# One encoder layer on one core: a new order at the head, one output bank moved, norm statistics and final outputs re-timed

## The chip, the cores and the metric

The kernel runs on one core of a Trainium2 chip. A core has a matrix engine (TensorE, PE in the profile; its weight loads are listed as PEld), a vector engine (VectorE, DVE), an activation engine (ScalarE, ACT), a general engine (GpSimd, POOL) and a queue engine that mostly issues transfers (SyncE, SP). Each engine carries out its own list of instructions in the order of that list. Engines wait for each other by semaphores. The metric is the time of one execution on the device in microseconds (us).

## The reference

One layer of an encoder over 512 tokens of width 2048, in float32, followed by a last norm:

```python
xn = rms_norm(x, attn_norm_g[l])
proj = jnp.einsum("bsd,dc->bsc", xn, w_in[l])
u_val, u_gate, q, k, v = jnp.split(proj, split_pts, axis=-1)
y_conv = conformer_conv(u_val, u_gate, conv_dw_w[l], conv_dw_b[l], conv_ln_g[l], conv_ln_b[l])
...
y_na = neighborhood_attention(heads(q), heads(k), heads(v), rpb[l])
mixed = jnp.concatenate([rms_norm(y_conv, conv_out_g[l]), rms_norm(y_na, na_out_g[l])], axis=-1)
x = x + jnp.einsum("bsc,cd->bsd", mixed, w_out[l])
xn = rms_norm(x, ffn_norm_g[l])
up = jnp.einsum("bsd,df->bsf", xn, w_up[l])
up = depthwise_conv(up, ffn_dw_w[l], ffn_dw_b[l])
gate, val = jnp.split(up, 2, axis=-1)
x = x + jnp.einsum("bsf,fd->bsd", jax.nn.silu(gate) * val, w_down[l])
...
return rms_norm(x, final_norm_g)
```

`conformer_conv` is a gated linear unit, a depthwise convolution of width 31, a LayerNorm over 1024 channels and a swish. `neighborhood_attention` has 16 heads of width 64 on an 8 x 64 grid of tokens, each token looking at an 8 x 16 window. The MLP has 5632 hidden channels and a depthwise convolution of width 3 in its middle.

## The kernel before

**Layout.** Activations lie with channels on the 128 partitions and the 512 tokens along the free axis: x is 16 tiles of 128 x 512 (`KD` = 16). Weights come as raw units of 128 x 1024 float32 (512 KB) on SP's queue. Each product is made of three matmuls of a faster float32 form (`mm3`, lines 127 to 129): the weights are split into a high part `whi` (ACT, L116) and a low part `wlo` (DVE, L117), the activations likewise, and PE adds high x high, high x low and low x high. A unit of weights has one of four buffers (`NW` = 4): the split of a new unit writes where the fourth unit before it was, so it waits until PE has done with that one. Raw units have seven buffers.

**Order.** The program is written stage by stage, and a scheduler sets the order of each engine's list by dependencies and priority. `pin` keeps marked instructions in program order. `tick` moves a generator on by one `yield` behind a given matmul: so the steps of a norm (sum of squares, statistics, broadcast) are spread between the products of the stage in which they run. What is written later has lower priority, but an engine's list is fixed when the program is built.

**Banks.** PE writes to eight PSUM banks of 128 x 512: three that rotate under the tag `mm` (pool `psm`), one with the tag `po`, two that rotate as `tr`, and a pair `sc`.

**The stages the change touches**, in order of time:

- *Head* (lines 93 to 96, 214 to 255). ACT's queue loads the norm's factors g1 from the parameter array. DVE sets `ones` and casts it to `warm`; PE runs 20 idle matmuls on it, eight of full height (L236) and twelve of 64 rows (L240). SP's queue loads x tiles (L247) with the first weights of two column tiles (value and gate) between them, in pieces (`piece`, L225): one transfer of each tile at a time, 128 KB each at first. Each x tile is scaled by its factors and split: xh on ACT (L249), xl on DVE (L250). Then `project_first` multiplies both tiles, 16 steps of six matmuls.
- *Conv norms* (`group_a`). After the sums of the LayerNorm come two ticks, then its statistics `rln`; then eight swish tiles, then `RA_AFTER` = 2 more ticks, then the statistics `ra` of the group's RMS norm. Statistics are `rsqrt_steps`: matmuls with ones sum over the partitions (st, L190), DVE and ACT form the root (rsv, rsr, rsy), DVE builds a diagonal matrix in two parts (dg: L197 the high part, L201 four pieces of the low one), and one broadcast matmul for each part (st, L207) gives the factor of every token in a bank, which ACT copies out (L211).
- *Output projection*, first half (`out_half(ma, read_a)`). 16 groups of 24 matmuls, each group in the next of the three `mm` banks. `read_a` multiplies a finished group by ra (oa, L585) and adds it to x (L586). Until ra is there, groups wait in their banks. The last attention steps run between the groups: scores, softmax, weighted sum, squares of the result added to `accna` (L170).
- *First up-projection tile* (`up_apart(0, ...)`). Seven products of 24 matmuls over half the tokens each, from sums of weight quarters (ws, L666 to L677) and of x halves, which make up a fast matrix multiplication. The first three products start together; their results are read by ACT (vv, L823) and DVE (vl, L825). Product 6 is in the `po` bank, the others are in `mm` banks. The statistics of the MLP's norm (`rstd2`) run between the products.
- *Tail* (lines 918 to 998). The last output is written in two parts. For 384 of the 512 tokens, channels stay on partitions: `finish` multiplies each of the 16 x tiles by its gain and the token's factor and stores pairs; ten tiles are done on DVE from the broadcast's bank (fin, L935), six on POOL from its copy rb (L966, L933). For the last 128 tokens PE transposes, so that tokens lie on partitions, in four groups of 512 columns, g0 to g3: ACT sums squares (sq, L981), DVE multiplies by the final gains (xg, L984), and when the last group is done the root is formed (`root`, line 173) and the four xg are scaled by it and stored (out_N, L998). `spread(g, k)` hands out the `finish` calls over the groups: one after each step from (1, 0) on. PE's list has the groups in the order g0, g2, g1, g3.

Of the kernel before, what the change touches and what calls it, by code (L numbers as in the profile page):

```python
# [10 lines left out]
F32 = mybir.dt.float32  # L11
# [5 lines left out]
P = 128  # L17
D = 2048
# [36 lines left out]
RA_AFTER = 2  # L55

PCOLS = [("g1", KD), ("dww", NC_ * CK), ("dwb", NC_), ("lng", NC_), ("lnb", NC_), ("cog", NC_),
# [10 lines left out]
def layer(ctx: ExitStack, tc: tile.TileContext, xT, xG, w_in, w_v, w_out, w_up, w_down, par, tab, g3, out, last_out):  # L68
# [27 lines left out]
    pin(nc.scalar.dma_start(g1, par[:, POFF["g1"]:POFF["g1"] + KD]))  # L96
# [5 lines left out]

    ones_r = consts.tile([P, P], F32R, name="ones")
# [112 lines left out]
    early = [[], []]  # L216

    def piece(u, j, c0, c1):

        if c0 == 0:  # L220
            early[j].append((t4([P, U * P], "raw"), wpool.tile([P, U * P], F32R, tag="whi", name="whi", bufs=NW),
                             wpool.tile([P, U * P], F32R, tag="wlo", name="wlo", bufs=NW)))
        n = (NC_, 0)[j]
        raw, hi, lo = (t[:, c0 * P:c1 * P] for t in early[j][u])
        pin(nc.sync.dma_start(raw, w_in[n, :, (u * U + c0) * P:(u * U + c1) * P]))  # L225
        pin(nc.scalar.activation(hi, raw, AF.Copy))
        pin(nc.vector.tensor_sub(lo, raw, hi.bitcast(F32)))
# [4 lines left out]
    warm = t2("warm", F32R)  # L232
    pin(nc.vector.tensor_copy(warm.rearrange("p (i k) -> p i k", k=P), ones.unsqueeze(1).broadcast_to([P, S // P, P])))
    ps = psa.tile([P, 2, S], F32, tag="sc", name="idle")
    for n in (S, S) + 3 * (H,) + 3 * (H - 32,):
        pin(nc.tensor.matmul(ps[:, 0, :n], warm[:, :P], warm[:, :n], start=True, stop=True))  # L236
    for n in (S, S) + 4 * (H,):
        for j in range(2):
            rows = slice(j * DH, (j + 1) * DH)
            pin(nc.tensor.matmul(ps[:, j, :n], warm[rows, :P], warm[rows, :n], start=True, stop=True))  # L240


    pieces = {k: [(u, j, c0, c1) for j in range(2)]
              for k, u, c0, c1 in ((0, 0, 0, 2), (2, 0, 2, 4), (4, 0, 4, 8), (6, 1, 0, 4), (9, 1, 4, 8))}
    for k in range(KD):
        x1.append(t2("x"))
        last = pin(nc.sync.dma_start(x1[k], xG[k]))  # L247
# [4 lines left out]
        for c in pieces.get(k, ()):  # L252
            piece(*c)
# [118 lines left out]
    def group_a():  # L372
# [26 lines left out]
        for _ in range(RA_AFTER):  # L399
            yield  # L400
# [672 lines left out]
```

## Time and profile before

| | |
|---|---|
| median of 3 runs | 2029.9 us (2029.69 to 2030.85) |
| profiled execution | 2030.16 us |
| its span in the trace | 2028.4 us |
| PE busy | 2015.4 us, 99%, 10672 instructions |
| DVE busy | 1675.5 us, 83% |
| ACT busy | 1050.9 us, 52% |
| POOL busy | 159.5 us, 8% |
| bytes moved | 276.41 MB, mean 136 GB/s |

How to read it: the span runs from the first to the last instruction of the profiled execution, and its own time has 1.8 us around it. Busy times of different engines overlap. An idle time of an engine matters only where the chain of work that ended last runs through it. A matmul's bar in the trace is longer than its share of the time, since matmuls overlap; what counts is the distance between starts (0.23 us for 512 columns, 0.12 us for 256).

### The profile page before, as it was taken

Reading aid. Unit: us, or ns where it says so; the run is one execution under the profiler, and the core shown is the slowest. Engines: PE = TensorE matmul, PEld = TensorE weight load, DVE = VectorE, ACT = ScalarE, POOL = GpSimd, SP = SyncE. Lnnn points to the kernel's source line nnn. Section 1 sums busy time; section 2 is a strip of 40 time slices with the busy share of each in tenths; the row PEclk is TensorE's granted clock in tenths of the full one; section 3 lists DMA queues with packets and bytes.
Section 4 is the critical chain, followed back from the end, with each engine's and each line's share of the span. In section 5 each row is a group of like instructions: output and inputs, shape, how many; then the busy total and the mean of one; then the engine's idle time right before and its main releaser. Section 6 shows DMA issues by size and latency. Waiting matters only on the chain.

```text
span 2028.4 us, 28313 instructions
## 1 busy us (share of the span) xinstructions
PE 2015.4 (99%) x10672; PEld 1726.5 (85%) x10672; DVE 1675.5 (83%) x2298; ACT 1050.9 (52%) x1674; POOL 159.5 (8%) x188
## 2 busy tenths in 40 slices
PE   9999999999999999999999999999999999999998
PEld 7888888888888998888888888888888888888887
DVE  7986888988577898888888888888888888889875
ACT  7323344466346555555555555555555555555563
POOL 0000000000001001111111111111111111110111
PEclk9999999999999999999999999999999999999999
DMA  7232333336347435566565565565565565564583
GB/s 256 83 104 84 114 94 109 109 124 215 108 120 178 120 114 146 123 147 146 125 146 146 128 142 146 128 142 146 121 149 146 125 146 146 127 144 127 144 206 126
DMA packets 97784, 276.41 MB, mean 136 GB/s; under 512 B 10992, under 2 KB 12784, under 8 KB 97648
## 3 DMA queue, kind: packets, MB, share of 16 engines
q1 hardware_dynamic: 72288, 228.45, 36.3%
q0 software_dynamic: 25216, 46.15, 15.5%
q8 instruction: 84, 1.38, 0.3%
q14 instruction: 52, 0.43, 0.1%
q10 hardware_dynamic: 144, 0.01, 0.0%
HBM read 220.04 MB, written 54.53 MB: 135 GB/s over the span
## 4 chain that ended last, share of the span: by engine, by line
PE 96%; DVE 2%; DMA 1%; ACT 0%; issue 0%; SPq 0%; ACTq 0%; DVEq 0%
PE pu L718 25%; PE pu L724 13%; PE pd L129 8%; PE pd L127 8%; PE pd L128 8%; PE pj L127 5%; PE pj L128 5%; PE pj L129 5%; PE po L127 3%; PE po L128 2%; PE po L129 2%; PE pv L313 1%; PE pv L312 1%; PE pv L314 1%; PE pu L127 1%; PE pu L129 1%
## 5 line engine op out<-in xcount | busy, mean ns | idle before, releaser
L116 ACT ACTIVATE whi<-raw 128x1024 fp32r<-128x1024 f32 x364 | 384.4, 1058 | 503.8 <-PE pj L128 136.6
L117 DVE TENSOR_TENSOR wlo<-raw,whi 128x1024 fp32r<-128x1024 f32 x364 | 444.4, 1221 | 214.0 <-ACT whi L116 205.2
L718 PE MATMUL pu<-xc,whi 128*128 128x512 f32 x2240 | 552.9, 391 | 0.0
L718 PEld LDWEIGHTS pu<-xc,whi 128*128 128x128 f32 x2240 | 413.0, 188 | 79.1
L724 PEld LDWEIGHTS pu<-xc,wlo 128*128 128x128 f32 x2240 | 292.3, 191 | 13.9
L724 PE MATMUL pu<-xc,wlo 128*128 128x256 f32 x2240 | 296.6, 283 | 0.0
L129 PE MATMUL pd<-hh,wlo 128*128 128x512 f32 x640 | 250.1, 391 | 0.0
L127 PE MATMUL pd<-hh,whi 128*128 128x512 f32 x640 | 249.6, 390 | 0.0
L128 PE MATMUL pd<-hl,whi 128*128 128x512 f32 x640 | 249.3, 390 | 0.0
L871 POOL DMA_DIRECT2D x2d<-pdc x160 | 139.4, 873 | 1162.4 <-ACT pdc L870 837.4
L128 PE MATMUL pj<-xl,whi 128*128 128x512 f32 x512 | 200.2, 391 | 0.1
L129 PE MATMUL pj<-xh,wlo 128*128 128x512 f32 x512 | 200.0, 391 | 0.0
L127 PE MATMUL pj<-xh,whi 128*128 128x512 f32 x512 | 198.9, 393 | 0.0
L750 ACT ACTIVATE pl<-pu 128x256 f32<-128x256 f32 x280 | 104.6, 382 | 143.5 <-PE pu L718 136.4
L116 ACT ACTIVATE whi<-ws 128x1024 fp32r<-128x1024 f32 x132 | 139.8, 1059 | 75.2 <-PE pu L718 58.2
L366 DVE SCALAR_TENSOR_TENSOR y<-ch,prm,y 128x500 f32<-128x500 f32 (+14 forms) x240 | 173.3, 740 | 4.3
L117 DVE TENSOR_TENSOR wlo<-ws,whi 128x1024 fp32r<-128x1024 f32 x132 | 161.1, 1220 | 13.9 <-ACT whi L116 13.6
L129 PEld LDWEIGHTS pd<-hh,wlo 128*128 128x128 f32 x640 | 120.1, 188 | 28.5 <-DVE wlo L117 3.3
L128 PEld LDWEIGHTS pd<-hl,whi 128*128 128x128 f32 x640 | 120.2, 188 | 24.9 <-DVE hl L856 0.3
L127 PEld LDWEIGHTS pd<-hh,whi 128*128 128x128 f32 x640 | 120.4, 188 | 22.6
L870 ACT ACTIVATE pdc<-pd 128x512 f32<-128x512 f32 x160 | 93.8, 588 | 79.3 <-PE pd L129 65.9
L127 PEld LDWEIGHTS pj<-xh,whi 128*128 128x128 f32 x512 | 96.3, 188 | 20.7 <-ACT xh L249 0.2
(204 smaller groups left out, 2886.4 us busy)
## 6 DMA issues: line engine op xcount, KB each, us to landing
raw<-in_w_up SPq DMA_DIRECT2D x176, 512.0 KB, 3.7
raw<-in_w_down SPq DMA_DIRECT2D x88, 512.0 KB, 4.0
x2d<-pdc POOLq DMA_DIRECT2D x160, 256.0 KB, 4.8
raw<-in_w_in SPq DMA_DIRECT2D x60, 512.0 KB, 3.8
raw<-in_w_out SPq DMA_DIRECT2D x32, 512.0 KB, 3.8
raw<-in_w_v SPq DMA_DIRECT2D x16, 512.0 KB, 4.1
tab<-in_tab SPq DMA_DIRECT2D x32, 256.0 KB, 5.0
x<-in_xG SPq DMA_DIRECT2D x16, 256.0 KB, 5.4
```

Of the source, the lines that this page charges most:

```text
L116: i = nc.scalar.activation(hi[:, :n], raw[:, :n], AF.Copy)
L117: j = nc.vector.tensor_sub(lo[:, :n], raw[:, :n], hi[:, :n].bitcast(F32))
L127: nc.tensor.matmul(ps, hi[:, a], mh, start=start, stop=False)
L128: nc.tensor.matmul(ps, hi[:, a], ml, start=False, stop=False)
L129: return nc.tensor.matmul(ps, lo[:, a], mh, start=False, stop=stop)
L312: nc.tensor.matmul(ps, xh, wh[:, f], start=kk == 0, stop=False)
L366: nc.vector.scalar_tensor_tensor(y[:, a:b], h[:, a + j - PAD:b + j - PAD], prm[:, o + j:o + j + 1], y[:, a:b], op0=ALU.mult, op1=ALU.add)
L718: i = nc.tensor.matmul(ps, w[0][:, k * P:(k + 1) * P], comb[c][k], start=k == 0, stop=stop and k == ks[-1])
L724: i = nc.tensor.matmul(ps[:, H:], w[1][:, k * P:(k + 1) * P], comb[c][k][:, :H], start=False, stop=stop and k == U - 1)
L750: nc.scalar.activation(to, ps, AF.Copy)
L870: nc.scalar.activation(t, ps, AF.Copy)
L871: nc.gpsimd.dma_start(xd[d], t, accum_op=ALU.add)
```

## The change

- *Head.* The factors g1 leave the parameter array and are put behind the first x tile, in one array `x0` with it; one transfer brings both, and a copy on DVE puts the factors in their place. The transfer on ACT's queue goes. The first weights of the two tiles are interleaved in a new array `w_a`, so that one transfer brings the same steps of both; the pieces are those of steps 0 to 1, 2 to 3, 4 to 7, 8 to 11 and 12 to 15, issued behind x tiles 0, 1, 3, 7 and 11. xh of the first x tile is made by DVE, the others by ACT as before. `warm` is set by a memset, and the 20 idle matmuls become seven of full height (six of 512 columns, one of 256).
- *Conv norms.* Three ticks instead of two before `rln`; none instead of two before `ra`.
- *First up-projection tile.* For f = 0 the product in the `po` bank is product 3 instead of product 6.
- *Tail.* The second step of the statistics and the copy rb move from (1, 0) to (2, 2); from then on `finish` is called twice at each step instead of once. Two instructions are pinned, with which the order of PE's list stays g0, g2, g1, g3. The sum over the first three groups stands ahead of xg of g2. The root is written out with one step fewer between the square root and its result.

The instruction lists change with it. On PE, 13 idle matmuls go, and every real matmul stays. In the conv-norm stage, 35 matmuls of the output projection stand between the last conv-norm product and the next attention scores, where there were 24, and the broadcast for ra stands among them; on DVE the split of the weights that follow, and the sum into accna, stand ahead of the first oa, where the first oa stood ahead of both the next split and the adds to x. In the first up-projection tile both broadcast matmuls of rstd2 stand together behind the second tile's first product; on DVE the split of one more unit stands between the two parts of dg. In the tail, DVE's list has xg of g0 and xg of g1 ahead of the first fin, then six fin, the sum, xg of g2, four fin; ACT's list has rb behind sq of g1. ACT has one more activation table load (19 instead of 18).

```diff
--- before.py
+++ after.py
@@ -52,9 +52,8 @@
 ORDER = "aavaav" + "aq" * 4 + "qqqq"
 NORM_AT = 4
 NG = GW // 8
-RA_AFTER = 2
-
-PCOLS = [("g1", KD), ("dww", NC_ * CK), ("dwb", NC_), ("lng", NC_), ("lnb", NC_), ("cog", NC_),
+
+PCOLS = [("dww", NC_ * CK), ("dwb", NC_), ("lng", NC_), ("lnb", NC_), ("cog", NC_),
          ("nag", NC_), ("g2", KD), ("fww", 2 * NF * 3), ("fwb", 2 * NF), ("g3", KD)]
 POFF = {}
 _o = 0
...
@@ -93,13 +92,14 @@
     pin = tc.keep_in_program_order
 
     g1 = consts.tile([P, KD], F32, name="g1")
-    pin(nc.scalar.dma_start(g1, par[:, POFF["g1"]:POFF["g1"] + KD]))
     prm = consts.tile([P, NPAR], F32, name="prm")
 
     def pc(name, i):
         o = POFF[name] + i
         return prm[:, o:o + 1]
 
+    warm = t2("warm", F32R)
+    pin(nc.vector.memset(warm.bitcast(F32), 1.0))
     ones_r = consts.tile([P, P], F32R, name="ones")
     ones = ones_r.bitcast(F32)
     nc.vector.memset(ones, 1.0)
@@ -213,44 +213,49 @@
 
     xs, x1 = [], []
     acc1 = t2("acc1")
-    early = [[], []]
-
-    def piece(u, j, c0, c1):
-
-        if c0 == 0:
-            early[j].append((t4([P, U * P], "raw"), wpool.tile([P, U * P], F32R, tag="whi", name="whi", bufs=NW),
-                             wpool.tile([P, U * P], F32R, tag="wlo", name="wlo", bufs=NW)))
-        n = (NC_, 0)[j]
-        raw, hi, lo = (t[:, c0 * P:c1 * P] for t in early[j][u])
-        pin(nc.sync.dma_start(raw, w_in[n, :, (u * U + c0) * P:(u * U + c1) * P]))
-        pin(nc.scalar.activation(hi, raw, AF.Copy))
-        pin(nc.vector.tensor_sub(lo, raw, hi.bitcast(F32)))
+    early = []
+    xg0 = t4([P, U * P], "raw")[:, :S + KD]
+    pin(nc.sync.dma_start(xg0, x0))
+
+    def piece(k0, k1):
+
+        if k0 % CH == 0:
+            early.append((t4([P, U * P], "raw"), wpool.tile([P, U * P], F32R, tag="whi", name="whi", bufs=NW),
+                          wpool.tile([P, U * P], F32R, tag="wlo", name="wlo", bufs=NW)))
+        o = k0 // CH * U * P
+        pin(nc.sync.dma_start(early[-1][0][:, 2 * k0 * P - o:2 * k1 * P - o], w_a[:, 2 * k0 * P:2 * k1 * P]))
+        by = 2 if k0 else 1
+        for k in range(k0, k1, by):
+            raw, hi, lo = (t[:, 2 * k * P - o:2 * (k + by) * P - o] for t in early[-1])
+            pin(nc.scalar.activation(hi, raw, AF.Copy))
+            pin(nc.vector.tensor_sub(lo, raw, hi.bitcast(F32)))
 
 
     idle = consts.tile([P, 1], F32, name="idle")
     pin(nc.scalar.activation(idle, ones[:, 0:1], AF.Square))
-    warm = t2("warm", F32R)
-    pin(nc.vector.tensor_copy(warm.rearrange("p (i k) -> p i k", k=P), ones.unsqueeze(1).broadcast_to([P, S // P, P])))
     ps = psa.tile([P, 2, S], F32, tag="sc", name="idle")
-    for n in (S, S) + 3 * (H,) + 3 * (H - 32,):
+    for n in 6 * (S,) + (H,):
         pin(nc.tensor.matmul(ps[:, 0, :n], warm[:, :P], warm[:, :n], start=True, stop=True))
-    for n in (S, S) + 4 * (H,):
-        for j in range(2):
-            rows = slice(j * DH, (j + 1) * DH)
-            pin(nc.tensor.matmul(ps[:, j, :n], warm[rows, :P], warm[rows, :n], start=True, stop=True))
-
-
-    pieces = {k: [(u, j, c0, c1) for j in range(2)]
-              for k, u, c0, c1 in ((0, 0, 0, 2), (2, 0, 2, 4), (4, 0, 4, 8), (6, 1, 0, 4), (9, 1, 4, 8))}
+
+    pieces = {0: (0, 2), 1: (2, 4), 3: (4, 8), 7: (8, 12), 11: (12, 16)}
     for k in range(KD):
-        x1.append(t2("x"))
-        last = pin(nc.sync.dma_start(x1[k], xG[k]))
+        if k:
+            x1.append(t2("x"))
+            last = pin(nc.sync.dma_start(x1[k], xG[k - 1]))
+        else:
+            x1.append(xg0[:, :S])
         h, l = t2("xh", F32R), t2("xl", F32R)
-        pin(nc.scalar.activation(h, x1[k], AF.Copy, scale=g1[:, k:k + 1]))
-        pin(nc.vector.scalar_tensor_tensor(l, x1[k], g1[:, k:k + 1], h.bitcast(F32), op0=ALU.mult, op1=ALU.subtract))
+        g = g1[:, k:k + 1] if k else xg0[:, S:S + 1]
+        if k:
+            pin(nc.scalar.activation(h, x1[k], AF.Copy, scale=g))
+        else:
+            pin(nc.vector.tensor_scalar(h, x1[k], g, None, op0=ALU.mult))
+        pin(nc.vector.scalar_tensor_tensor(l, x1[k], g, h.bitcast(F32), op0=ALU.mult, op1=ALU.subtract))
         xs.append((h, l))
-        for c in pieces.get(k, ()):
-            piece(*c)
+        if k in pieces:
+            piece(*pieces[k])
+        if k == 0:
+            pin(nc.vector.tensor_copy(g1, xg0[:, S:]))
     with tc.issue_after(last.ins):
         nc.sync.dma_start(prm, par)
     a_, q_, v_ = iter(range(NC_)), iter(range(NP_)), iter(range(2))
@@ -331,7 +336,7 @@
         both = [psa.tile([P, S], F32, tag="tr", name="pj", bufs=2) for _ in range(2)]
         for kk in range(KD):
             for j in range(2):
-                m = mm3(both[j], early[j][kk // U][1:], kk % U, xs[kk][0], xs[kk][1], kk == 0, kk == KD - 1)
+                m = mm3(both[j], early[kk // CH][1:], kk % CH * 2 + j, xs[kk][0], xs[kk][1], kk == 0, kk == KD - 1)
             if kk % 4 == 3:
                 tick(m)
         return both
@@ -385,8 +390,8 @@
             sum_sq(acc, ys[i], i == 0)
             if i == NC_ // 2 - 1:
                 yield
-        yield
-        yield
+        for _ in range(3):
+            yield
         r = yield from rsqrt_steps(acc, CONV, "rln")
         acc = t2("acc")
         for i in range(NC_):
@@ -396,8 +401,6 @@
             sum_sq(acc, ys[i], i == 0)
             if i % 2:
                 yield
-        for _ in range(RA_AFTER):
-            yield
         ra.append((yield from rsqrt_steps(acc, CONV, "ra")))
 
 
@@ -793,7 +796,7 @@
     def up_apart(f, between):
 
         def begin(c):
-            return weights(), (psa.tile([P, S], F32, tag="po", name="pu") if c == 6 else
+            return weights(), (psa.tile([P, S], F32, tag="po", name="pu") if c == (6 if f else 3) else
                                psm.tile([P, S], F32, tag="mm", name="pu"))[:, :H]
 
         def part(c, w, ps, ks):
@@ -956,38 +959,45 @@
     def spread(g, k):
         if (g, k) == (0, 1):
             next(stats)
-        elif (g, k) == (1, 0):
+        elif (g, k) == (2, 2):
             try:
                 next(stats)
             except StopIteration as e:
                 rb.append(e.value)
-            finish(pairs.pop(0), rb[0], split=True)
             rb.append(t2("rb")[:, fm])
             nc.scalar.activation(rb[1], rb[0], AF.Copy)
-        elif rb and pairs:
-            at = pairs.pop(0)
+        for at in pairs[:2 if rb else 0]:
+            pairs.remove(at)
             finish(at, rb[at % 3 == 1], at % 3 == 1, at % 3 != 1)
 
     for g, ps in enumerate(banks):
         for i in range(CH):
-            nc.tensor.matmul(ps[:, i * P:(i + 1) * P], x2[g * CH + i][:, tm], ident, start=i == 0, stop=False,
-                             is_transpose=True)
+            m = nc.tensor.matmul(ps[:, i * P:(i + 1) * P], x2[g * CH + i][:, tm], ident, start=i == 0, stop=False,
+                                 is_transpose=True)
+            if g == CH - 1 and i == 0:
+                pin(m)
         for k in range(n):
             (hh, hl), (dh, dl) = hs[k], ws[g * CH + k]
-            nc.tensor.matmul(ps, hh[:, tm], dh, start=False, stop=False)
+            i = nc.tensor.matmul(ps, hh[:, tm], dh, start=False, stop=False)
+            if (g, k) == (2, 3):
+                pin(i)
             nc.tensor.matmul(ps, hl[:, tm], dh, start=False, stop=False)
             nc.tensor.matmul(ps, hh[:, tm], dl, start=False, stop=k == n - 1)
             spread(g, k)
         nc.scalar.activation(t2("sq"), ps, AF.Square, accum_out=sums[:, g:g + 1])
+        if g == CH - 2:
+            nc.vector.tensor_reduce(v, sums[:, :CH - 1], axis=AX.X, op=ALU.add)
+            nc.vector.tensor_scalar(v, v, 1.0 / D, EPS, op0=ALU.mult, op1=ALU.add)
         xg.append(t2("xg"))
         if g < CH - 1:
             nc.vector.tensor_mul(xg[g], ps, gains[g])
-        if g == CH - 2:
-            nc.vector.tensor_reduce(v, sums[:, :CH - 1], axis=AX.X, op=ALU.add)
-            nc.vector.tensor_scalar(v, v, 1.0 / D, EPS, op0=ALU.mult, op1=ALU.add)
     assert not pairs
     nc.vector.scalar_tensor_tensor(v, sums[:, CH - 1:], 1.0 / D, v, op0=ALU.mult, op1=ALU.add)
-    root(r, y, v)
+    nc.scalar.activation(r, v, AF.Sqrt)
+    nc.vector.tensor_scalar(v, v, -0.5, None, op0=ALU.mult)
+    nc.vector.reciprocal(r, r)
+    nc.vector.scalar_tensor_tensor(y, r, v, r, op0=ALU.mult, op1=ALU.mult)
+    nc.vector.scalar_tensor_tensor(y, y, 1.5, r, op0=ALU.add, op1=ALU.mult)
     for g in range(CH):
         if g == CH - 1:
             nc.vector.scalar_tensor_tensor(xg[g], banks[g], y, gains[g], op0=ALU.mult, op1=ALU.mult)
@@ -1016,8 +1026,10 @@
     a = {n: np.asarray(v) for n, v in inputs.items()}
     xT = np.ascontiguousarray(a["x"][0].T).reshape(KD, P, S)
     xG = np.ascontiguousarray(xT.reshape(KD, P, WH, NG, 8).transpose(0, 1, 3, 2, 4)).reshape(KD, P, S)
+    x0, xG = np.concatenate([xG[0], _cols(a["attn_norm_g"][0])], axis=1), np.ascontiguousarray(xG[1:])
     wi = a["w_in"][0]
     w_in = np.ascontiguousarray(_units(wi[:, :2 * CONV + 2 * NA]))
+    w_a = np.stack([w_in[n].reshape(P, KD, P) for n in (NC_, 0)], axis=2).reshape(P, -1)
     w_v = np.ascontiguousarray(wi[:, 2 * CONV + 2 * NA:].reshape(KD // 2, 2, P, 2, S).transpose(3, 0, 2, 1, 4)
                                ).reshape(2, KD // 2, P, 2 * S)
     wo = a["w_out"][0]
...
```

More of the change, by code (lines that the diff above doesn't have):

```diff
@@ L67, in layer @@
 @with_exitstack
-def layer(ctx: ExitStack, tc: tile.TileContext, xT, xG, w_in, w_v, w_out, w_up, w_down, par, tab, g3, out, last_out):
+def layer(ctx: ExitStack, tc: tile.TileContext, xT, xG, x0, w_a, w_in, w_v, w_out, w_up, w_down, par, tab, g3, out, last_out):
     nc = tc.nc
@@ L1058 @@
     tab = np.ascontiguousarray(tab.transpose(0, 2, 1, 3))
-    arrays = {"xT": xT, "xG": xG, "w_in": w_in, "w_v": w_v, "w_out": w_out, "w_up": w_up, "w_down": w_down,
+    arrays = {"xT": xT, "xG": xG, "x0": np.ascontiguousarray(x0), "w_a": np.ascontiguousarray(w_a), "w_in": w_in, "w_v": w_v, "w_out": w_out, "w_up": w_up, "w_down": w_down,
               "par": np.ascontiguousarray(par), "tab": tab,
```

1 line of the change is left out of this document (removed).

## The prediction

> **What bounds the kernel now.** I read the page first, then all waits of the matmul engine, then the timeline at each of them.
>
> ```profile
> span 2028.4 us, 28313 instructions
> PE 2015.4 (99%) x10672; PEld 1726.5 (85%) x10672; DVE 1675.5 (83%) x2298; ACT 1050.9 (52%) x1674; POOL 159.5 (8%) x188
> PE 96%; DVE 2%; DMA 1%; ACT 0%; issue 0%; SPq 0%; ACTq 0%; DVEq 0%
> ...
> PE idle L236 <- DVE warm L233: 1.6, 1, 1.6
> PE pu L127 <- ACT vv L823: 1.5, 1, 1.5
> PE st L190 <- DVE acc L170: 0.3, 1, 0.3
> PE po L127 <- DVE oa L585: 0.3, 1, 0.3
> ```
>
> The chain that ends last is 96% TensorE (PE), and PE is busy 99% of the span. The change drops 13 idle matmuls and no real one, so it can gain only at the start, in PE's few waits (1.5, 0.3 and 0.3 us after the start) and behind PE's last matmul. Against that, each wait that a new instruction order makes on PE lengthens the run in full. So I laid the changed kernel's order on each engine against the old one and walked through the four places where they differ, with durations of the old trace. The profiled execution took 2030.16 us (1.8 us around its span); the median of the runs is 2029.9, 0.26 less. 0.2% of it, 4.1 us, is about what a measurement here can tell from no change: "same" means 2025.8 to 2034.0.
>
> **The head.** Columns of a timeline: start, duration, engine, line, operation; in brackets the engine's idle time and what ended it.
>
> ```profile
> 1.65 2.47 PE L236 MATMUL idle<-warm 128*128 128x512 f32 x8 [1.65 <-DVE warm L233]
> ...
> 4.39 0.40 ACT L226 ACTIVATE whi<-raw 128x256 fp32r<-128x256 f32 x1
> ...
> 5.52 0.42 ACT L226 ACTIVATE whi<-raw 128x256 fp32r<-128x256 f32 x1 [0.73 <-DMA raw<-in_w_in]
> ...
> 6.05 0.80 PE L127 MATMUL pj<-xh,whi 128*128 128x512 f32 x1
> 6.64 0.63 PE L128 MATMUL pj<-xl,whi 128*128 128x512 f32 x1
> 7.07 0.63 PE L129 MATMUL pj<-xh,wlo 128*128 128x512 f32 x1
> 7.50 0.51 PE L127 MATMUL pj<-xh,whi 128*128 128x512 f32 x1
> 7.85 0.39 PE L128 MATMUL pj<-xl,whi 128*128 128x512 f32 x1
> 8.08 0.40 PE L129 MATMUL pj<-xh,wlo 128*128 128x512 f32 x1
> ```
>
> The first real matmul (6.05) waits for the second tile's first weights: they land at 5.5, the first tile's by 4.39. Matmul starts lie 0.59, 0.43, 0.43 and 0.35 us apart, then 0.23: PE runs at half speed until about 7.7, six microseconds after its first idle matmul. Now both tiles' first weights come in one 256 KB transfer, directly behind the x tile that brings its factors along. I bound its landing by these two rows, so the first real matmul starts between 6.05 - 1.13 = 4.92 and 6.05. Started at 4.92 with the switch still at 7.7, 1.13 us of half-speed work is won, worth half, 0.6. If the denser idle matmuls also bring the switch ahead of all real work, the excess of the four gaps over 0.23 (0.36 + 0.20 + 0.20 + 0.12 = 0.9) goes too: 1.13 + 0.9 = 2.0 won. In the other direction, seven idle matmuls (about 0.59 + 5 x 0.43 + 0.2 = 2.9 us from 1.4) end at 4.3, and PE pauses. If the six microseconds counted from the first real matmul, half speed would last to 10.9 or 12.1 instead of 7.7: 1.0 to 2.2 lost. I take **-0.6**, the case nearest to the rows (-2.0 to +2.2). The factor transfer that goes from ACT's queue, the cast that becomes a memset and xh of the first tile moving to DVE all lie in the time in which PE runs idle matmuls; uncovered, the last would add 0.7.
>
> **Conv norms and output projection.** One more tick before the first conv norm (rln) removes the wait of L190 (0.3). Without RA_AFTER the second one's factor (ra) is ready before the projection's second group, where it was read late.
>
> ```profile
> 497.83 0.58 ACT L507 ACTIVATE ao<-po 128x512 f32<-128x512 f32 x1
> 498.44 0.63 ACT L169 ACTIVATE sq<-ao 128x512 f32<-128x512 f32 x1
> 499.11 0.69 DVE L170 TENSOR_TENSOR accna<-accna,sq 128x512 f32<-128x512 f32 x1 [0.25 <-ACT sq L169]
> 500.47 1.29 DVE L585 TENSOR_TENSOR oa<-po,ra 128x512 f32<-128x512 f32 x2 [0.67 <-ACT ra L211]
> 500.57 0.39 PE L129 MATMUL po<-mah,wlo 128*128 128x512 f32 x1
> 500.77 1.06 ACT L116 ACTIVATE whi<-raw 128x1024 fp32r<-128x1024 f32 x1 [0.33 <-PE po L128]
> 501.22 0.50 PE L127 MATMUL po<-mah,whi 128*128 128x512 f32 x1 [0.26 <-DVE oa L585]
> 503.48 1.21 DVE L117 TENSOR_TENSOR wlo<-raw,whi 128x1024 fp32r<-128x1024 f32 x1
> ```
>
> PE's fourth output group (501.22) takes the bank of the first, which DVE frees with oa. In the old order oa stands ahead of the next weight split, at 500.47, and PE waits 0.26. In the new order eleven more projection matmuls stand ahead of the next attention step's scores, which come 11 x 0.23 = 2.5 us later, and DVE has that step's softmax, then wlo, then accna, and only then oa. This wlo belongs to weights whose buffer (four in turn) is the one that the third group has just used. So nothing on that path can start before PE finishes the third group: whi 1.06, wlo 1.21, accna 0.69 (its square follows whi by 0.58 + 0.63, as late as wlo), oa 0.69, together 3.65, less about 0.3 of overlap, plus hand-overs: **3.5** of wait on PE, with the rest of PE's list behind it. Lower bound 0, if the buffers came free another way. Less the 0.3 and 0.3 removed: **+2.9** (-0.6 to +3.2). The moved statistics themselves (st, dg, st) end 1 to 2 us ahead of PE by the same walk. One more activation table load lies on ACT, busy 52%.
>
> **First up-projection tile.**
>
> ```profile
> 678.80 0.28 PE L129 MATMUL pu<-xc,wlo 128*128 128x256 f32 x1
> ...
> 680.61 0.39 PE L127 MATMUL pu<-xc,whi 128*128 128x256 f32 x1 [1.53 <-ACT vv L823]
> ...
> 693.11 0.28 PE L127 MATMUL pu<-xc,whi 128*128 128x256 f32 x1
> 693.44 0.47 PE L207 MATMUL st<-dg,ones 128*128 128x512 f32 x1
> ...
> 694.35 1.13 DVE L201 SCALAR_TENSOR_TENSOR dg<-ident,rsy,dg 128x128 fp32r<-128x128 f32 x4
> ...
> 695.66 0.40 PE L207 MATMUL st<-dg,ones 128*128 128x512 f32 x1
> ```
>
> Product 3 gets a bank that is free, so the gap of 678.80 to 680.61 shrinks to the usual 0.12: 1.69 won. In the old order PE reaches the first broadcast (st) at 693.2, waits 0.2, and the second stands 16 matmuls behind it, which covers L201. In the new order both stand together at the end of the second tile's first product, about 694.1 (23 matmuls later, 1.9 sooner), and on DVE another wlo stands between the two factors (dg). Its whi needs the buffer of that very product: from its end run whi 1.06, wlo 1.21, L201 1.13, about 3.4 with the hand-over, before PE may do the second st; the first st fills 0.23 of it, some 1.5 us in, since L197 stands behind three splits and two weight sums. Cost 3.2, less 1.69 and 0.2: **+1.3** (-1.9 to +2.5).
>
> **The clock in these waits.** Windows: columns are busy time with counts of PE, PEld, DVE, ACT, POOL, then the granted clock.
>
> ```profile
> 2019.40:2021.50 2.10, 0.00 (x0) 0.00 (x0) 1.58 (x9) 0.86 (x3) 1.00 (x2) 1.00 1.02 380
> 2021.60:2028.40 6.80, 0.00 (x0) 0.00 (x0) 1.17 (x3) 1.34 (x2) 0.00 (x0) 0.50 0.79 295
> ```
>
> About 2.2 us after PE's last matmul its clock fell to half; the old waits, up to 1.5, were shorter. A 3.5 us wait is longer than that, and by the head it may take up to six microseconds of work to leave half speed: 0 to 3.0 lost. I take half of it for the unbroken wait, **+1.5**, and **+0.8** for the broken one (pieces of 1.5 and 1.7 us), 0 to 3.0 each. The Trainium skill, "TensorE: Matmul & The Clock Gate", Part 1, has the clock fall only after a whole idle window of about 3.4 us, of a free-running grid. By that rule a 3.5 us wait would seldom hold such a window and the clock term would be nearly 0, which is the second rival below; the row has it fall after 2.2.
>
> **The tail.**
>
> ```profile
> 2012.77 1.14 DVE L935 SCALAR_TENSOR_TENSOR fin<-x,prm,st 128x384 f32<-128x384 f32 x2 [0.87 <-PE st L207]
> 2014.52 5.88 POOL L933 TENSOR_TENSOR fin<-x,rb 128x384 f32<-128x384 f32 x6 [39.61 <-ACT rb L966]
> 2016.51 0.60 ACT L981 ACTIVATE sq<-pt 128x512 f32<-128x512 f32 x1 [2.07 <-PE pt L979]
> 2017.23 0.69 DVE L984 TENSOR_TENSOR xg<-pt,g3b 128x512 f32<-128x512 f32 x1
> 2017.84 1.66 DVE L935 SCALAR_TENSOR_TENSOR fin<-x,prm,st 128x384 f32<-128x384 f32 x3
> 2020.45 0.16 DVE L989 SCALAR_TENSOR_TENSOR rsv<-rsl,rsv 128x1 f32<-128x1 f32 x1
> 2021.66 0.49 DVE L997 TENSOR_SCALAR xg<-xg,rsy 128x512 f32<-128x512 f32 x1
> ```
>
> Ten fin outputs run on DVE, from 2012.77 on, six on POOL, from 2014.52. In the new order xg of group g1 stands on DVE ahead of all of them, and it needs PE's end of g1 (2016.5, where sq starts); on ACT rb, which POOL needs, stands behind that sq. So DVE stands still from about 2012 to 2016.5. Then: xg to 2017.1, six fin at 0.54 to 2020.4, reduce and xg of g2 to 2021.2, four fin to 2023.4, then the root, which loses one small step (0.2): 1.21 - 0.2 = 1.0 from the variance to L997, so L997 starts at 2024.4, **+2.8**. POOL, started at 2017.7, ends by 2023.6 and isn't later. What follows L997 I leave as it was. Lower bound -0.2 (fin hidden after all), upper +3.5 (outputs bunch in the queues).
>
> **Sum.** -0.6 + 2.9 + 1.3 + 1.5 + 0.8 + 2.8 = +8.7 on 2030.16 gives 2038.9, against the median 2038.6.
>
> **Rivals.**
> - *The order does no harm* (the splits and fin come in time, as they did): -0.6 - 0.6 - 1.9 - 0.2 = -3.3, **2026.6**; with the best head 2025.2. For it: the old kernel's lists, of the same length, cost PE 2 us in all. Against it: in both stages the wait closes on itself, since the split ahead needs PE's latest product.
> - *The clock holds*: the same without the clock terms, +6.4, **2036.3**.
> - *One of the three costs is absent* (tail, bank or broadcast): +8.7 less 2.8, 5.0 or 4.0, **2033.4 to 2035.6**.
> - *Slower still: half speed lasts.* Each wait costs the full 3.0, and the head's pause adds 2.2 in place of -0.6: **2045**. It decides if the clock needs the whole six microseconds anew.
> - *The change doesn't do what it says at the head*: the common transfer lands no sooner than 5.5; +0.6, **2039.2**, which the forecast's range holds.
>
> **How the numbers follow.** Forecast with its near range (2036.5 to 2042, the slow head in it) 0.47; clock holds 0.17; one cost absent 0.15; no harm 0.13; half speed lasts 0.08. The range of 2031.5 to 2043.5 leaves out most of "no harm" and of the last one, about 0.2. Slower than 2034.0: 0.47 + 0.17 + 0.08 + half to two thirds of 0.15, about 0.81; faster only with the best head in "no harm", 0.04; same 0.15.
>
> **What would show it.** PE waits of about 3.5 us at a projection matmul near 500 us with oa as releaser, and at a broadcast st near 694 with dg as releaser; no wait on vv near 679; matmul starts 0.4 apart behind either wait if the clock falls; the first fin on DVE behind an xg, five microseconds after its st; the first real matmul at 4.9 to 6.0. I'm wrong if PE's waits add up to under 3 us, or if the last outputs leave no later after PE's last matmul than now.

## The result and the profile after

The changed kernel takes 2040.51 us (median of 6 runs, 2039.91 to 2041.58), beside 2030.38 for the old one on the same chip (6 runs, 2029.69 to 2030.85): a ratio of 1.005, 95% interval 1.0037 to 1.0063, so about 10 us slower. Beside the experiments further down, 27 of 90 runs of the old kernel took 2031.2 to 2034.3 us and the others 2029.3 to 2030.7, so the means of its runs lie 0.5 to 0.8 above their medians. The profiled execution of the changed kernel took 2040.10 us, with this span, these busy times and this chain of work (the page of the changed kernel):

```profile
span 2038.3 us, 28283 instructions
PE 2016.6 (99%) x10659; PEld 1727.7 (85%) x10659; DVE 1676.5 (82%) x2299; ACT 1050.1 (52%) x1673; POOL 159.6 (8%) x188
PE 97%; DVE 1%; DMA 1%; issue 0%; SPq 0%; ACT 0%; ACTq 0%
```

The summary looks like that of the old kernel: PE is still 99% busy, and it is 1.2 us more busy although 13 idle matmuls are gone. The loss of 9.9 us in the span can't be read here. It shows in PE's waits (engine, its line, what it waited for: us in total, times, longest):

```profile
engine line waited for: us in total, times, longest us
PE po L127 <- DVE oa L588: 3.4, 1, 3.4
PE st L207 <- DVE dg L201: 1.6, 1, 1.6
PE idle L238 <- DVE warm L102: 1.5, 1, 1.5
PE st L207 <- DVE dg L197: 1.4, 1, 1.4
PE pj L127 <- ACT whi L230: 0.4, 1, 0.4
```

The wait on vv (1.5) and the two of 0.3 are gone; in their place stand 3.4 behind oa, and 1.4 + 1.6 behind the two halves of dg. Where the time goes along the run is seen by counting PE's real matmuls in both traces and comparing the starts of those that have equally many before them:

| | before, us | after, us | after - before |
|---|---|---|---|
| first real matmul | 6.05 | 4.98 | -1.07 |
| with 48 before it | 18.29 | 17.64 | -0.65 |
| with 2650 before it, behind the moved ra | 529.24 | 532.18 | +2.94 |
| with 3700 before it, behind the first up-projection tile | 719.76 | 725.43 | +5.67 |
| last | 2018.94 | 2024.62 | +5.68 |
| end of the span | 2028.39 | 2038.33 | +9.94 |

So there are four terms: the head -0.65, the conv-norm stage +3.6, the first up-projection tile +2.7, and what lies behind PE's last matmul +4.3. Between them nothing moves: the 1300 us of MLP behind the 3700 matmuls add 0.01. Here is each place in the timeline of the changed kernel, in selected rows (start, duration, engine, line, operation, idle time and releaser). The head:

```profile
1.46 3.14 PE L238 MATMUL idle<-warm 128*128 128x512 f32 x7 [1.46 <-DVE warm L102]
...
4.51 0.72 ACT L230 ACTIVATE whi<-raw 128x256 fp32r<-128x256 f32 x2 [2.27 <-DMA raw<-in_w_a]
4.98 0.80 PE L127 MATMUL pj<-xh,whi 128*128 128x512 f32 x1 [0.38 <-ACT whi L230]
```

The common transfer has landed by 4.5; real work starts 1.07 us sooner, and PE's idle matmuls end only 0.38 before it. The conv-norm stage:

```profile
499.01 0.39 PE L129 MATMUL po<-mah,wlo 128*128 128x512 f32 x1
499.21 1.06 ACT L116 ACTIVATE whi<-raw 128x1024 fp32r<-128x1024 f32 x1 [0.98 <-PE po L128]
500.18 0.58 ACT L510 ACTIVATE ao<-po 128x512 f32<-128x512 f32 x1
500.30 1.22 DVE L117 TENSOR_TENSOR wlo<-raw,whi 128x1024 fp32r<-128x1024 f32 x1 [0.60 <-ACT whi L116]
500.79 0.63 ACT L169 ACTIVATE sq<-ao 128x512 f32<-128x512 f32 x1
501.45 0.69 DVE L170 TENSOR_TENSOR accna<-accna,sq 128x512 f32<-128x512 f32 x1
502.06 1.28 DVE L588 TENSOR_TENSOR oa<-po,ra 128x512 f32<-128x512 f32 x2
502.80 0.79 PE L127 MATMUL po<-mah,whi 128*128 128x512 f32 x1 [3.40 <-DVE oa L588]
503.39 0.63 PE L128 MATMUL po<-mal,whi 128*128 128x512 f32 x1
503.81 0.63 PE L129 MATMUL po<-mah,wlo 128*128 128x512 f32 x1
```

The factor ra itself has been ready since 486.3 (L211). Read from top to bottom this is the loop: PE ends the third group; that frees a weight buffer for whi; wlo follows whi; accna follows its square, which stands behind whi on ACT; oa follows accna; and oa frees the bank that PE needs. Behind the wait the matmuls start 0.59 and then 0.43 apart instead of 0.23. The first up-projection tile:

```profile
697.03 0.28 PE L129 MATMUL pu<-xc,wlo 128*128 128x256 f32 x1
697.28 1.06 ACT L116 ACTIVATE whi<-ws 128x1024 fp32r<-128x1024 f32 x1 [1.82 <-PE pu L128]
697.84 0.68 DVE L197 TENSOR_TENSOR dg<-ident,rsy 128x512 fp32r<-128x512 f32 x1
698.45 1.22 DVE L117 TENSOR_TENSOR wlo<-ws,whi 128x1024 fp32r<-128x1024 f32 x1
698.67 0.47 PE L207 MATMUL st<-dg,ones 128*128 128x512 f32 x1 [1.36 <-DVE dg L197]
699.58 1.13 DVE L201 SCALAR_TENSOR_TENSOR dg<-ident,rsy,dg 128x128 fp32r<-128x128 f32 x4
700.77 0.79 PE L207 MATMUL st<-dg,ones 128*128 128x512 f32 x1 [1.63 <-DVE dg L201]
```

The split (698.45) stands between the two parts of dg, and its whi (697.28) waited for the very product that has just ended. And the tail, with PE's broadcast (L207) and rows of DVE, ACT, POOL and SP's queue:

```profile
2016.88 0.68 DVE L993 TENSOR_TENSOR xg<-pt,g3b 128x512 f32<-128x512 f32 x1
2017.39 0.51 PE L207 MATMUL st<-dg,ones 128*128 128x384 f32 x2
...
2021.84 0.60 ACT L987 ACTIVATE sq<-pt 128x512 f32<-128x512 f32 x1 [6.06 <-PE pt L985]
2022.43 0.48 ACT L968 ACTIVATE rb<-st 128x384 f32<-128x384 f32 x1
2022.56 0.69 DVE L993 TENSOR_TENSOR xg<-pt,g3b 128x512 f32<-128x512 f32 x1 [5.00 <-ACT sq L987]
2023.00 5.83 POOL L936 TENSOR_TENSOR fin<-x,rb 128x384 f32<-128x384 f32 x6 [42.09 <-ACT rb L968]
2023.17 3.23 DVE L938 SCALAR_TENSOR_TENSOR fin<-x,prm,st 128x384 f32<-128x384 f32 x6
2023.80 0.87 SPq L940 DMA_DIRECT2D out_T<-fin  x2
...
2030.27 0.49 DVE L1007 TENSOR_SCALAR xg<-xg,rsy 128x512 f32<-128x512 f32 x1
2030.65 0.45 SPq L942 DMA_DIRECT2D out_T<-fin  x1
...
2031.19 2.83 SPq L1008 DMA_DIRECT2D out_N<-xg  x4
```

The factor of the tokens is in its bank at 2017.9, but DVE stands still for 5.0 us until it can do the xg of g1, and ACT for 6.06 until its square; the first fin starts at 2023.17. L1007 (L997 of the old kernel) starts 5.65 us after PE's last matmul instead of 2.72.

### The profile page after: what moved, and what is told of

Read it like the earlier page. It is cut to its first block, busy times and chain, and to the rows that moved or that the text cites. A ratio compares the mean times of both kernels' runs of the same rounds, so it can differ in the third digit from the quotient of the medians.

```text
span 2038.3 us, 28283 instructions
## 1 busy us (share of the span) xinstructions
PE 2016.6 (99%) x10659; PEld 1727.7 (85%) x10659; DVE 1676.5 (82%) x2299; ACT 1050.1 (52%) x1673; POOL 159.6 (8%) x188
## 4 chain that ended last, share of the span: by engine, by line
PE 97%; DVE 1%; DMA 1%; issue 0%; SPq 0%; ACT 0%; ACTq 0%
PE pu L721 25%; PE pu L727 13%; PE pd L129 8%; PE pd L127 8%; PE pd L128 8%; PE pj L127 6%; PE pj L129 6%; PE pj L128 6%; PE po L127 3%; PE po L128 3%; PE po L129 3%; PE pv L317 1%; PE pv L319 1%; PE pv L318 1%; PE pu L127 1%; PE pu L128 1%
```

## The experiments

Each kernel below is the old one with the part of the change that is named, unless it says otherwise. Ratios are against the old kernel, run in turn with it on the same chip.

**Each part alone.** First the head: all of its hunks, with the old statistics, banks and tail.

> Only the head of the change, on the kernel before. My theory: the common weight transfer lands about 1 us sooner and half of that is kept, so 0.6 to 0.7 us less than the kernel before, with the first real matmul near 5.0 and the half-speed matmuls ending between 7 and 8 us. Rival (what was gained at the first matmul is lost to the pause behind the idle matmuls): no gain, half speed until 10 us or later. No wait on oa or dg in either case.

Measured: 2030.03 us beside 2030.01, ratio 0.9997 (0.9987 to 1.0006). In its trace PE's last matmul starts 1.16 us sooner than before, yet the span is 0.3 us shorter only. What PE gains is given back behind it: 10.34 us from PE's last matmul to the end, 9.45 before. Two things make up the 0.9. The last stores land later after their issue (the very last one 3.58 instead of 3.04); these rows of the transfers (KB each, median us to landing) are those of the old kernel and of this one:

```profile
out_N<-xg SPq DMA_DIRECT2D x4, 256.0 KB, 3.2
```

```profile
out_N<-xg SPq DMA_DIRECT2D x4, 256.0 KB, 3.6
```

And after the last landing the program needs 1.33 us to its end instead of 0.97.

Then the bank of the first up-projection tile:

```diff
-            return weights(), (psa.tile([P, S], F32, tag="po", name="pu") if c == 6 else
+            return weights(), (psa.tile([P, S], F32, tag="po", name="pu") if c == (6 if f else 3) else
```

> Only the bank of product 3, on the kernel before. My theory (the split ahead of the low dg closes the wait on itself): the 1.7 us gap near 679 goes, two waits before the broadcasts near 697 add 3.4, and the clock may fall behind them for one spell of 3.4 us, costing up to 1.5: 1.2 to 2.9 us more than before. Rival (those waits come from the earlier ra, not from the bank): the gap goes and nothing comes, 1.7 to 1.9 us less than before.

Measured: 2033.33 beside 2030.01, ratio 1.0011 (1.0001 to 1.002); span 2030.8, 2.4 more than before. Two of its waits on PE:

```profile
PE st L207 <- DVE dg L201: 1.6, 1, 1.6
PE st L207 <- DVE dg L197: 1.4, 1, 1.4
```

The same 1.6 and 1.4 as with the whole change, and no wait on vv. So the bank alone makes the new order at the broadcasts, and the later arrival from the conv-norm stage has no part in it.

Then the later place of ra's statistics, `RA_AFTER = 2` to `RA_AFTER = 0`:

> Only RA_AFTER = 0, on the kernel before. My theory: one wait of 3.4 us before the fourth output group with oa as releaser, in place of 0.3, and half speed behind it for up to 3 us (1.5 lost): 3.1 to 4.7 us more than before. The small wait of the first norm's statistics stays. Rival (the third tick is needed for it): less than 0.5 us of change.

Measured: 2034.68 beside 2030.01, ratio 1.0018 (1.0009 to 1.0027). Its longest wait on PE:

```profile
PE po L127 <- DVE oa L585: 3.4, 1, 3.4
```

The 3.4 us come from removing the two ticks alone. Behind this wait half speed held twice as long in the profiled execution as in the full change (see the last section). That execution took 2035.92, 1.2 more than the median; the median's 4.7 above the old kernel is close to what the wait and a spell as long as the full change's would make (3.40 - 0.26 + 1.47 = 4.6).

Then the tail's hunk (statistics and rb at (2, 2), two `finish` calls a step, the sum ahead of xg, the shorter root):

> Only the tail of the change, on the kernel before. My theory: DVE stands still until PE ends group g1, so from PE's last matmul to the end it takes 13.7 us as in the changed kernel, against 9.4 before: 4.3 us more. Rival (the time before the tail matters, since the weights and x tiles then arrive otherwise): less than 3 us more.

Measured: 2033.96 beside 2030.01, ratio 1.0017 (1.0007 to 1.0026); from PE's last matmul to the end 12.77 us instead of 9.45, so +3.3. The same kernel once more:

> e4 once more, for one look at the same kernel beside the others: the end comes 12.8 us after PE's last matmul starts, against 9.4 before.

Measured: 2033.12 in one run, and 12.8 us again. The profiled execution of e4 took 2036.81 for a reason ahead of the tail, in code that e4 leaves as it was: a weight transfer held DVE until 675.12 (673.36 in the old kernel's trace), PE waited 0.66 for xc and 2.33 for vv (1.53 in the old kernel's trace), and half speed followed from 683.78 to 687.19. The full change has 13.71 behind PE's last matmul; the 0.9 that the tail doesn't make is the 0.9 of the head.

The four parts alone cost 0.0, 3.3, 4.7 and 3.95 us by their medians, 12 together; the whole change costs 10.1. By the means of all runs the parts cost -0.4, 2.7, 4.3 and 3.8, together 10.4 beside 10.2. None of the four holds the third tick ahead of rln, which wasn't run alone; at its place the changed kernel gains 0.7 (see the account of the prediction). So the difference in the medians is no sign that the parts act on each other.

**Is it the order on DVE, at the broadcasts?** The old kernel with the bank change, in which the split that came between the two parts of dg is held back behind the second part:

```diff
+        if dg_first:
+            with tc.issue_after(dg_first.pop().ins):
+                j = nc.vector.tensor_sub(lo[:, :n], raw[:, :n], hi[:, :n].bitcast(F32))
...
+        if free:
+            dg_first.append(low)
```

> Bank of product 3 as in e2, and the first weight split that is written behind the statistics of rstd2 is held behind both parts of dg on DVE. My theory (the split between the parts of dg closes the wait): no wait of PE over 0.5 us at the two broadcasts, no half speed near 700 us, the gap near 679 gone: 1.2 to 1.9 us less than the kernel before. Rival (the moved bank delays the broadcasts whatever the order): waits of 1 us or more at st stay, no gain.

Measured: 2030.47 beside 2030.33, ratio 0.9999 (0.999 to 1.0009). Its largest waits on PE behind the start:

```profile
PE pu L135 <- DVE wlo L123: 0.9, 1, 0.9
PE pu L133 <- ACT whi L118: 0.4, 1, 0.4
```

Both waits at st are gone, and so are the 3 us: the split ahead of L201 was their cause. But the 1.5 us of the old wait on vv, gone as well, aren't won. The splits come late, and PE waits 0.9 and 0.4 for them some ten microseconds on. DVE is busy 9.97 of the 10 us from 690 to 700 in this trace: a split held back there is late, and PE's wait only moves.

**Why does the head's gain not arrive?** One part of the answer lies ahead of the end, and the traces kept show it: nine executions have the old head (the old kernel, e2 to e6, e9, e11, e12) and five the new one as it stands or nearly so (the changed kernel, e1, e7, e8, e10). The first real matmul starts at 5.57 to 6.05 us with the old head and at 4.98 to 5.12 with the new one, but the matmul with 48 before it starts at 17.63 to 18.29 (mean 17.93) and at 17.11 to 18.31 (mean 17.59). Beside the spread of one head, 0.7 and 1.2 us, the gain of 0.3 is not shown; the old kernel's own trace is the latest of its nine. By the means of all their runs e1, e7 and e10 are 0.4, 0.6 and 0.7 us shorter than the old kernel beside them, also within the noise.

The other part lies at the end. The first theory was the closing of the program: SP waits for semaphores of outstanding transfers one after another, and the head issues six transfers fewer (five of them on SP's queue), so that the last store falls on another place in the rotation of eight. The head again, with the load of the parameters cut into seven transfers:

```diff
-        nc.sync.dma_start(prm, par)
+        cut = [NPAR * i // 7 for i in range(7 + 1)]
+        for c0, c1 in zip(cut, cut[1:]):
+            nc.sync.dma_start(prm[:, c0:c1], par[:, c0:c1])
```

> The head alone as in e1, with the load of prm cut into seven transfers, so that SP issues as many transfers as the kernel before and the last store has the same place in the rotation of eight semaphores. My theory (what the head won is lost again at the end, since the closing waits begin with the one that comes last): from the last landing to the end 0.97 us again instead of 1.33, and 0.4 to 0.9 us less than e1. Rival (the stores are slower because the arrays lie elsewhere in memory): the last four stores land 3.5 us after their issue as in e1, and the closing takes what it takes: less than 0.4 us of difference to e1.

Measured: 2030.26 beside 2030.33, ratio 0.9994 (0.9985 to 1.0004). The time after the last landing is back at 0.97, so the closing's 0.36 does depend on the number of transfers: behind the last landing SP's trace has two semaphore waits in the old kernel and in e7, and eight, 0.06 us apart, in e1. The stores still take 3.50 to 3.76 us; and the median is no better than that of e1 (2030.03).

For the slower stores two causes were tried. The first, that ACT's queue no longer takes part: the head, with g1 loaded by a transfer on ACT's queue again.

```diff
+    pin(nc.scalar.dma_start(g1, x0[:, S:]))
...
-        if k == 0:
-            pin(nc.vector.tensor_copy(g1, xg0[:, S:]))
```

> The head alone as in e1, but g1 comes from x0 by a transfer of its own on ACT's queue, as it came from the parameter array before, and not by DVE's copy. Theory A (the stores at the end are slower where the queue of ACT is never used): they land 3.0 to 3.4 us after their issue, and the kernel takes 0.4 us less than e1 at the end. Theory B (they are slower because of where the arrays lie): 3.5 to 3.8 us as in e1.

Measured: 2030.32 beside 2030.45, ratio 0.9997 (0.9988 to 1.0007); the last stores took 3.46, 3.76, 3.52 and 3.56 us. Not this. The second, that other arrays lie in memory: the old kernel with x0 and w_a as further inputs that nothing reads.

> The kernel before with the two new arrays x0 and w_a among its inputs, behind the others, but never read. Theory B (place of the arrays): the last four stores land 3.5 to 3.8 us after their issue. Theory A (the queue): 3.0 to 3.4 us as in the kernel before. Everything else as before.

Measured: 2030.23 in one run; the stores took 3.19, 3.37, 3.12 and 3.07, as in the old kernel. Not this either, as it was tried; arrays that lie between the others, and are read, were not tried. Why the same stores land 0.3 to 0.6 us later in kernels with the new head stays open.

**What of the tail costs?** The tail as changed, but with the statistics' second step and rb at (1, 0) as in the old kernel:

```diff
-        elif (g, k) == (2, 2):
+        elif (g, k) == (1, 0):
...
-        for at in pairs[:2 if rb else 0]:
+        for at in pairs[:2 if (g, k) >= (2, 2) else 0]:
```

> The tail of the change as in e4, but the second step of the statistics and the copy rb stay at (1, 0); two finish calls at each step from (2, 2) on, the sum ahead of xg of g2 and the shorter root as in the change. My theory (DVE stands still because every fin waits behind xg of g1, and POOL because rb waits behind sq of g1): fin starts again within a microsecond of the broadcast and the end comes 9.2 to 9.7 us after PE's last matmul, so -0.3 to +0.3 us against the kernel before. Rival (two finish calls at a time, all late, are what delays the outputs): 11 us or more after PE's last matmul, 2 to 3.3 us more than before.

Measured: 2029.33 beside 2030.45, ratio 0.9992 (0.9982 to 1.0001). Its timeline in the tail:

```profile
2012.19 0.49 ACT L965 ACTIVATE rb<-st 128x384 f32<-128x384 f32 x1 [2.62 <-PE st L207]
2012.71 3.77 DVE L935 SCALAR_TENSOR_TENSOR fin<-x,prm,st 128x384 f32<-128x384 f32 x7 [1.37 <-ACT rb L965]
...
2020.68 0.48 DVE L1004 TENSOR_SCALAR xg<-xg,rsy 128x512 f32<-128x512 f32 x1
```

The first fin starts at 2012.71, right behind rb, and from the start of PE's last matmul 8.78 us pass to the end, instead of 9.45 (old) and 12.8 (tail as changed). So the move of the statistics' second step and rb to (2, 2) costs 4.0, of which the other edits of the tail (the sum ahead of xg, the shorter root, the outputs in other steps) bring back 0.7. The same kernel again, in five rounds:

> e9 again, in five rounds, as the version that the runs point to. Theory: 0.5 to 1.2 us less than the kernel before and about 11 us less than the changed one, with the end 8.7 to 9.0 us after PE's last matmul. Rival (the median of e9 came from undisturbed first matmuls, not from the tail): no difference to the kernel before, and 9.4 us after PE's last matmul.

Measured: 2029.39 beside 2030.12, ratio 0.9997 (0.9988 to 1.0006); 8.79 us behind PE's last matmul. The trace gives the same 0.7 twice, the interval of the runs holds 1: the gain is shown in the profile, and not beyond the noise of the total. It is the best version found, about 11 us better than the changed kernel.

**The parts that seemed free of cost, together**: the head of e7, the held-back split of e5, and of the tail only the sum and the root.

> Head with seven transfers for prm as in e7, bank with dg first as in e5, and from the tail only the shorter root and the sum ahead of xg of g2; ticks, RA_AFTER and the finish calls as before. My theory adds the parts: -0.7 from the head, -1.9 from the bank, -0.2 from the root: 2.0 to 2.8 us less than the kernel before, about 2027.5. Rival (the parts are lost to outputs that end with the queue): less than 1 us of gain.

Measured: 2030.82 beside 2030.33, ratio 0.9999 (0.999 to 1.0009). No gain: its waits of 0.9 and 0.4 behind the held-back splits stay, its stores take 3.53 to 3.77 us, and in its profiled execution PE left half speed at 9.76 us only. From the start of PE's last matmul 9.92 us pass, beside 9.96 in e7, which has neither the sum nor the root of the new tail; so the 0.7 of e9 comes for the most part from the outputs in other steps.

## Why the prediction was right, and where its sizes were off

The direction and the size hold: +8.7 us forecast on the profiled execution, +9.94 measured, and the waits, their releasers and the first fin are where the forecast put them. Its sums hold but for one rival (one cost absent), where 2038.6 less 5.0 or 2.8 is 2033.6 to 2035.8 and not 2033.4 to 2035.6. Term by term:

- *The wait of the fourth output group.* Forecast 3.5 (whi, wlo, accna, oa in a loop through PE's third group), measured 3.40, in that order of instructions; e3 has it from its cause alone. Right. The rival "the order does no harm" falls with it.
- *The broadcasts.* Forecast 3.2 of wait, of which 1.69 and 0.2 stood in the old kernel too; measured 1.36 + 1.63 = 2.99, and the gap near 679 gone. Right, and e2 and e5 show the cause: it comes with the bank and goes with the split. The forecast named 694 us as the place and the timeline shows 697 to 701; that is the delay of the stage before (e2, without it, has the two matmuls at 695.11 and 697.20).
- *The clock.* Forecast +1.5 behind the unbroken wait and +0.8 behind the broken one. In both places the granted clock fell to half for 3.41 us, in which PE did 2.94 us of work: half of it, 1.47, is lost in each. The first term is right; the second is 0.7 too small, since I let a wait in two pieces count for half. The rival "the clock holds" falls.
- *The head.* Forecast -0.6 from 1.13 us of half-speed work; measured 1.07 us and -0.65 at PE in this one pair of traces. The agreement at PE is in part luck: the step took the end of half speed at 7.7 for a property of the kernel, and in nine executions of the same head it came at 4.92 to 7.94, and PE's place behind 48 matmuls spreads by 0.7. The step also took it that what PE gains there reaches the end. e1 shows that it doesn't: the new head also makes the last store 0.5 us later and the closing 0.36 us longer.
- *The tail.* Forecast L997 2.8 us later, measured 2.93, by the path given: DVE and ACT stand behind the end of g1. "What follows L997 I leave as it was" is the step that failed, and the largest miss of the sum: 6.73 us from there to the end became 8.06. 0.9 of these 1.3 come with the head (e1, and e4 without them); about 0.4 come from the queue of outputs, in which a fin store stood ahead of the last four until 2031.1, so that the first of them was issued 0.92 us after L1007 (2030.27 to 2031.19) instead of 0.52 (2021.66 to 2022.18).

By places: the conv-norm stage was forecast at 2.9 + 1.5 = 4.4 and took 3.6. Where both kernels have done the same matmuls, the changed one stands at -0.68 ahead of rln's statistics (2050 matmuls), -1.42 behind them (2150), -1.66 ahead of the wait (2370) and +2.94 behind it (2650). So the wait and the clock cost 4.60, as 3.40 + 1.47 - 0.26 says, and 1.0 was won ahead of them, of which the vanished wait of L190 is 0.31; the other 0.7 comes with the new order there, e1 with its old ticks doesn't have it, and its cause stays open. The up-projection tile was forecast at 1.3 + 0.8 = 2.1 and took 2.7, the clock's difference. The tail was forecast at 2.8 and took 4.3. So the near agreement of the sums is in part two misses of opposite sign.

## What to carry to other kernels

When a change moves an instruction in front of another on an in-order engine, ask of the one in front what it needs: if it needs a buffer that the waiting engine has only just released, the wait closes on itself and costs the whole chain (here four instructions, 3.4 us), though each engine has idle time. Removing a wait of 1.5 us by giving a product another bank brought nothing even with the order mended, since the engine behind it had no slack; look for the limit of the stretch first. And work that feeds the last outputs (here the fin products on DVE and the copy rb on ACT) must not stand behind work that ends late: nothing follows that could hide the delay (4.0 us, e4 beside e9). A gain of a few tenths at the start can't be read from one pair of traces: take several executions of each kernel first.

## What the runs showed of the hardware

*The clock falls and rises on a fixed grid.* The windows of the changed kernel, cut at the times at which its granted clock changes (busy time of PE, PEld, DVE, ACT, POOL; granted clock, DMA share, GB/s):

```profile
498.92:502.33 3.41, 0.48 (x3) 0.06 (x1) 2.77 (x5) 2.17 (x3) 0.00 (x0) 1.00 0.87 330
502.33:505.74 3.41, 2.94 (x7) 2.37 (x8) 3.38 (x6) 0.00 (x0) 0.00 (x0) 0.50 0.44 154
696.89:700.30 3.41, 0.89 (x5) 0.40 (x3) 3.41 (x6) 1.06 (x1) 0.00 (x0) 1.00 0.50 154
700.30:703.71 3.41, 2.94 (x13) 2.83 (x13) 3.41 (x8) 1.16 (x2) 0.00 (x0) 0.50 0.02 7
```

The two spells of half speed last 3.41 us each, and all changes in one trace are whole multiples of 3.41 us apart. This agrees with the free-running window of about 3.4 us that the Trainium skill gives in "TensorE: Matmul & The Clock Gate", Part 1. What it says of the fall does not agree: the window need not be idle as a whole. In the window ahead of the first fall PE was busy 0.48 of 3.41 us, ahead of the second 0.89, in pieces on both sides of the st. So a wait broken in two drops the clock like an unbroken one. The border lies near half: in e2 the clock fell behind a window 52% busy (1.78 of 3.41 us), and in e9, around the old wait on vv, it held behind one 55% busy (1.89 of 3.42). The rise asks for more than that: windows of e3, the ra part alone.

```profile
503.34:506.75 3.41, 2.64 (x6) 2.16 (x7) 3.38 (x7) 0.00 (x0) 0.00 (x0) 0.50 0.57 189
506.75:510.16 3.41, 3.41 (x9) 2.65 (x8) 0.43 (x1) 0.00 (x0) 0.00 (x0) 0.50 0.00 0
```

Here the window behind the wait was 2.64 of 3.41 us busy (77%), and half speed went on for a second one; 2.94 (86%) was enough above. In the head, a window busy for 2.91 of 3.42 us (e8) didn't end half speed, and one busy for 2.92 of 3.41 (e1) did. By these two traces, whether a wait of 3.4 us costs another 1.5 or 3 us behind it is a matter of where the grid falls.

*The end of half speed in the head differs from one execution of a kernel to the next.* By the granted clock it came at 7.94 and 4.92 us in e4 and e6, which are the same kernel, and at 5.95 and 7.67 in e9 and e12, which are too. With the old head all nine came between 4.92 and 7.94; with the new one it was 7.39 in the changed kernel and 4.38, 4.44, 4.76 and 9.76 in e1, e7, e10 and e8. So the idle matmuls alone don't set it.

*The closing of the program has a price of its own.* After the last landing 0.97 us passed with 503 transfers issued on the queues of SP and ACT (old kernel, e7), 1.33 with 497 (e1, the changed kernel) and 1.27 with 498 (e10); one transfer cut in seven moved it back from 1.33 to 0.97. The semaphores of these transfers rotate in eight, and SP waits for two, eight or seven of them behind the last landing, 0.06 us each.
